# The last block's FFN up projection by seven Strassen products in place of eight, with operands over the mixer's tiles

## The chip, the cores and the metric

One core of one Trainium2 chip. The metric is the device time of one execution in microseconds (us). TensorE (PE) multiplies, PEld is its weight load, VectorE (DVE), ScalarE (ACT) and GpSimd (POOL) work elementwise, SyncE (SP) issues the DMAs.

## What is computed

A hybrid layer for 2048 prompt tokens and 32 tokens of a running stream: input projection, stick-breaking attention beside an SSD scan, an output projection, and a convolutional FFN. The change touches the part after the output projection:

```python
def layer(x, ..., p):
    m, ... = mixer(rmsnorm(x, p['g_mix_pre']), ..., p)      # ends in  @ p['w_out']
    x = x + rmsnorm(m, p['g_mix_post'])
    f, ... = conv_ffn(rmsnorm(x, p['g_ffn_pre']), ffn_conv_prev, p)
    x = x + rmsnorm(f, p['g_ffn_post'])

def conv_ffn(h, conv_prev, p):
    gu = h @ p['w_up']                                      # 1024 -> 2 * 2816
    gate, up = gu[..., :D_FF], gu[..., D_FF:]
    gate_c, conv_new = causal_dwconv(gate, conv_prev, p['ffn_conv_w'], p['ffn_conv_b'])   # width 3
    act = jax.nn.gelu(gate_c, approximate=True) * up
    return act @ p['w_down'], conv_new
```

## The kernel before

Tokens run in four blocks of 512, 512, 512 and 544 (`SBS`; the last has 512 prompt tokens and the 32 of the stream), channels on the 128 partitions. Each fp32 operand is a pair of fp32r tiles, hi (a cast) and lo (the rest, by a subtraction). `dense` (L126) makes a product of 128 by 128 weights with three matmuls: hi with hi, hi with lo, lo with hi. The matmuls of the last block have 272 columns (two token halves), those of the others 512.

After `phase_in` (projections and SSD, all blocks), attention runs block by block, and the work that follows it for block s, `Tail.stream(s)`, is spread as filler between the attention steps of block s + 1; the order on PE is pinned there (`pin`, `mark`). The last block's stream runs alone (`alone`), unpinned, with PSUM pools `t` (3 banks) and `o` (2) and extra pools for loads and weights.

`stream` (L1117) goes so: `out_units` for the first token half, then for the second with steps of `residual(a)` in between (every fourth); `root(a)`; `residual(b)`; `split` of both halves; `root(b)`; the `owed` last downs of the block before; and then 22 pairs `up(s, j)` with `down` after each group of three (four in the last group of the last block). `residual` normalises the projected tile `m` and adds x; the squares for the next root are added on POOL (`square`, L782). `split` makes hi (ACT, L981) and lo (DVE, L982) of the operand with the gain but without the root r; `up` multiplies the gate's and the up half's sums by r (L1015 for the gate). So the matmuls do not wait for the root.

`up` issues 8 x 3 matmuls per token tile for the gate tile j and as many for the up tile 22 + j, so 96 of 272 columns in the last block. Between them stand the convolution and GELU: scale (ACT, L1026), two taps (DVE, L1028), Square (ACT, L1033), a product (DVE, L1034), Sigmoid (ACT, L1035), a product (POOL, L1036); then the product with up (DVE, L1045), and ah (ACT, L1050) and al (POOL, L1051) for the downs. In the last block two small DMAs (`o_fconv`) store the convolution's new state out of the tile `gb`, and the Square overwrites that tile.

`weight` (L97) makes hi and lo of a weight tile of 128 x 1024 in block 0 out of a raw load (`wraw`; ACT cast L110, POOL subtraction L111), and stores both to DRAM (L114, `wS_...`, 1 MiB); later blocks recall them with a DMA (L106). There are two raw tiles (`RBUFS`) and three weight tiles (`WBUFS`). SP issues its DMAs in order, and each waits for the one eight before it.

Of the kernel before, what the change touches and what calls it, by code (L numbers as in the profile page):

```python
# [18 lines left out]
STORE = True  # L19
WBUFS = 3  # L20
RBUFS = 2

P = 128
# [37 lines left out]
class Kernel:  # L61
# [35 lines left out]
    def weight(self, pool, src, n=KC, key=None, tag=None):  # L97

        nc = self.nc
        w = pool.tile([P, 2, KC, P], F32R, name=tag or "w", bufs=1 if tag else self.wbufs)  # L100
        hi, lo = w[:, 0], w[:, 1]
        keys = key if isinstance(key, list) else [key]
        if keys[0] in self.kept:
            m = n // len(keys)
            for i, k in enumerate(keys):
                nc.sync.dma_start(w[:, :, m * i : m * i + m, :].bitcast(F32), self.kept[k][:])  # L106
            return hi, lo
        raw = self.wp.tile([P, KC, P], F32, name="wraw", bufs=RBUFS)
        nc.sync.dma_start(raw[:, :n, :], src)
        nc.scalar.copy(hi[:, :n, :], raw[:, :n, :])  # L110
        nc.gpsimd.tensor_tensor(lo[:, :n, :], raw[:, :n, :], hi[:, :n, :].bitcast(F32), op=ALU.subtract)  # L111
        if key is not None and STORE:
            d = self.kept[key] = self.dp.tile([P, 2, n, P], F32, name="wS_" + "_".join(map(str, key)))
            nc.sync.dma_start(d[:], w[:, :, :n, :].bitcast(F32))  # L114
        return hi, lo
# [4 lines left out]
    def dense(self, ps, w, x, c0, c1, ks=KC, k0=0, first=True, last=True, pin=False):  # L120
        nc = self.nc
        (whi, wlo), (xhi, xlo) = w, x
        at = lambda t, k: t[k] if isinstance(t, list) else t[:, k, :]
        for k in range(ks):
            for i, (l, r) in enumerate(((whi, xhi), (whi, xlo), (wlo, xhi))):
                mm = nc.tensor.matmul(  # L126
                    ps[:, : c1 - c0],
                    l[:, k, :],
                    at(r, k0 + k)[:, c0:c1],
                    start=first and i == 0 and k == 0,  # L130
                    stop=last and i == 2 and k == ks - 1,
# [26 lines left out]
    def rstd_steps(self, pool, psp, pt, sq, n, width, tag="rstd", out=None, rcol=None, of=None, stay=False):  # L158
# [7 lines left out]
        for b in range(nb):  # L166
            q = min(P, n - b * P)
            for i, t in enumerate(sq):
                nc.tensor.matmul(
                    ps[:q, b : b + 1], t[:, b * P : b * P + q], self.ones[:, 0:1],  # L170
                    start=i == 0, stop=i == len(sq) - 1,
                )
# [446 lines left out]
class Attention:  # L619
# [172 lines left out]
    def heads(self, s, steps, every=None):  # L792
# [55 lines left out]

        def values():


            while late:
                h, kc, p, wt, v = late.pop()
                if kc == s and p == 0:
# [469 lines left out]
```

## Time and profile before

| what | us |
|---|---|
| runs: median (lowest to highest) | 2937.53 (2934.23 to 2947.28) |
| profiled execution: span of the core | 2945.7 |
| PE busy in it | 2816.0 (96%) |
| DVE, ACT, POOL busy | 1696.8, 1250.6, 1273.1 |
| mean granted TensorE clock | 0.978 of full |
| DMA | 586.36 MB, mean 199 GB/s |

The times come from separate runs, the profile from one execution of its own; its span is the time from the first instruction to the last, and nothing else is known of that execution's time. Stretches of the span are read as busy time per engine; "the chain of waits" follows back from what ended last.

### The profile page before, as it was taken

The page shows a single profiled execution, that of the slowest core. Times are in us where ns is not written, and L with a number is a line of the kernel's source. Part 1 is how long each engine was busy: PE and PEld are TensorE (multiplying, and loading weights), DVE is VectorE, ACT ScalarE, POOL GpSimd, SP SyncE. Part 2 cuts the span into 40 slices and gives each one's busy share as a digit, 9 for nine tenths or more (in the row PEclk, how much of TensorE's full clock was granted, in tenths as well). Part 3 has the DMA queues.
Part 4 walks back from the last instruction along what each step waited for, and adds up shares of the span by engine and source line. Part 5 has one row for each costly group of instructions (what it writes and reads, how often), then busy time and mean ns, then how long its engine had stood idle before and what let it go on. Part 6 is the DMA issues. An engine that isn't in the chain of part 4 may idle for free.

```text
span 2945.7 us, 44837 instructions
## 1 busy us (share of the span) xinstructions
PE 2816.0 (96%) x16699; PEld 2427.4 (82%) x16699; DVE 1696.8 (58%) x2628; ACT 1250.6 (42%) x2534; POOL 1273.1 (43%) x1083
## 2 busy tenths in 40 slices
PE   8999999989889999999999999999999999999997
PEld 6777787977778888888788888978888889899997
DVE  7667576557774555537644455786666652623333
ACT  4344444337665444436433334664444443311111
POOL 4565555435676656547422222553223234511113
PEclk9999999989999999999999999999999999999998
DMA  5646463648677777777555556656554445755555
GB/s 179 183 143 187 145 173 120 173 131 271 223 266 246 267 266 251 271 261 249 194 190 182 179 171 212 247 175 219 179 175 165 167 160 200 242 183 172 170 183 194
DMA packets 251308, 586.36 MB, mean 199 GB/s; under 512 B 66154, under 2 KB 107762, under 8 KB 222546
## 3 DMA queue, kind: packets, MB, share of 16 engines
q1 hardware_dynamic: 251090, 583.49, 59.9%
q8 instruction: 133, 2.18, 0.3%
q14 instruction: 85, 0.70, 0.1%
HBM read 445.70 MB, written 137.69 MB: 198 GB/s over the span
## 4 chain that ended last, share of the span: by engine, by line
PE 74%; DVE 12%; DMA 7%; ACT 2%; issue 2%; POOL 1%; SPq 1%; DVEq 0%; POOLq 0%; ACTq 0%
PE o L126 36%; PE u L126 12%; PE t L126 11%; PE z L821 4%; PE pa L862 4%; PE pt L840 3%; PE o L370 2%; DVE xc L346 2%; DMA acB<-acD 1%; DVE prow L672 1%; DMA w<-wS_out 1%; DVE acB L446 1%; DVE xc L342 1%; DVE x L268 1%; DMA xr<-hS 1%
## 5 line engine op out<-in xcount | busy, mean ns | idle before, releaser
L126 PE MATMUL o<-xhi,w 128*128 128x512 f32 (+2 forms) x3968 | 1047.4, 346 | 30.1 <-ACT xhi L292 7.7
L126 PEld LDWEIGHTS o<-xhi,w 128*128 128x128 f32 x3968 | 698.2, 192 | 124.2 <-ACT xhi L292 7.7
L126 PE MATMUL o<-xlo,w 128*128 128x512 f32 (+2 forms) x1984 | 683.8, 345 | 6.9 <-DVE xlo L278 4.2
L111 POOL TENSOR_TENSOR w<-wraw,w 128x1024 fp32r<-128x1024 f32 (+2 forms) x156 | 369.0, 2366 | 228.2 <-ACT w L110 207.1
L677 POOL TENSOR_TENSOR beta<-beta,prow 128x512 f32<-128x512 f32 (+3 forms) x256 | 255.0, 998 | 429.1 <-DVE prow L672 345.5
L126 PEld LDWEIGHTS o<-xlo,w 128*128 128x128 f32 x1984 | 380.5, 192 | 51.7 <-DVE xlo L278 6.1
L1036 POOL TENSOR_TENSOR y<-y,gb 128x512 f32<-128x512 f32 (+1 forms) x88 | 115.8, 1317 | 544.4 <-ACT gb L1035 544.4
L126 PE MATMUL u<-xhi,w 128*128 128x512 f32 x1056 | 349.4, 398 | 0.0
L126 PE MATMUL o<-ah,w 128*128 128x512 f32 x992 | 342.5, 403 | 3.1 <-DVE f L1082 3.0
L845 DVE TENSOR_TENSOR wt<-pt,wt 128x512 fp32r<-128x512 f32 (+2 forms) x320 | 191.7, 602 | 156.5 <-ACT wt L844 153.9
L672 DVE TENSOR_TENSOR_SCAN prow<-gam,prow,z 128x513 f32<-128x513 f32 x192 | 245.3, 1277 | 61.5 <-ACT beta L670 58.9
L844 ACT CAST wt<-pt 128x512 fp32r<-128x512 f32 (+2 forms) x320 | 167.5, 526 | 208.7 <-PE pt L840 207.1
L126 PEld LDWEIGHTS u<-xhi,w 128*128 128x128 f32 x1056 | 199.1, 189 | 46.6
L126 PEld LDWEIGHTS o<-ah,w 128*128 128x128 f32 x992 | 187.5, 189 | 45.4 <-DVE f L1082 3.9
L669 ACT ACTIVATE gam<-z 128x512 f32<-128x512 f32 (+2 forms) x320 | 173.3, 542 | 95.5 <-PE z L821 69.8
L126 PE MATMUL u<-xlo,w 128*128 128x512 f32 x528 | 209.4, 397 | 0.0
L110 ACT CAST w<-wraw 128x1024 fp32r<-128x1024 f32 (+2 forms) x156 | 155.2, 995 | 124.7 <-PE o L126 91.3
L1028 DVE SCALAR_TENSOR_TENSOR y<-gb,cv,y 128x512 f32<-128x512 f32 (+1 forms) x176 | 160.0, 910 | 69.2 <-ACT y L1026 66.3
L126 PE MATMUL o<-al,w 128*128 128x512 f32 x496 | 196.8, 397 | 0.0
L126 PE MATMUL t<-xhi,w 128*128 128x272 f32 x960 | 189.1, 292 | 1.7 <-DMA w<-wS_out 1.3
L840 PE MATMUL pt<-ident,beta 128*128 128x128 f32 x1088 | 183.2, 279 | 7.7 <-DVE rn_v L178 4.4
L862 PE MATMUL pa<-wt,v 128*64 128x256 f32 (+3 forms) x1152 | 176.2, 283 | 12.5 <-DVE wt L845 6.9
(269 smaller groups left out, 5086.3 us busy)
## 6 DMA issues: line engine op xcount, KB each, us to landing
w<-wS_up SPq DMA_DIRECT2D x132, 1024.0 KB, 4.8
w<-wS_dn SPq DMA_DIRECT2D x72, 768.0 KB, 4.8
wS_up<-w SPq DMA_DIRECT2D x44, 1024.0 KB, 4.8
w<-wS_out SPq DMA_DIRECT2D x39, 1024.0 KB, 6.7
wraw<-wup SPq DMA_DIRECT2D x44, 512.0 KB, 5.8
k<-kS SPq DMA_DIRECT2D x80, 256.0 KB, 4.3
v<-vS SPq DMA_DIRECT2D x80, 256.0 KB, 4.2
wS_dn<-w SPq DMA_DIRECT2D x24, 768.0 KB, 4.5
```

Source lines behind the costliest of these rows:

```text
L110: nc.scalar.copy(hi[:, :n, :], raw[:, :n, :])
L111: nc.gpsimd.tensor_tensor(lo[:, :n, :], raw[:, :n, :], hi[:, :n, :].bitcast(F32), op=ALU.subtract)
L126: mm = nc.tensor.matmul(ps[:, : c1 - c0], l[:, k, :], at(r, k0 + k)[:, c0:c1], start=first and i == 0 and k == 0, stop=last and i == 2 and ...
L669: nc.scalar.activation(g[:, c0:512], z, AF.Sigmoid, scale=-0.125)
L672: nc.vector.tensor_tensor_scan(back(pr), back(g), z[:, 0:1].to_broadcast([P, n + 1]), self.kn.ones[:, 0:1] if prev is None else prev, op0= ...
L677: eng.tensor_tensor(b[:, :n], b[:, :n], pr[:, c0 + 1 : 513], op=ALU.mult)
L821: mm = nc.tensor.matmul(z[:, :n], q[:, P * b : P * b + P], k[:, :n], start=e == 0, stop=e == 1 and kc < s)
L840: mm = nc.tensor.transpose(t[:, P * j : P * j + P], w[:, P * j : P * j + P], kn.ident[:])
L844: nc.scalar.copy(hi, t)
L845: nc.vector.tensor_tensor(lo, t, hi.bitcast(F32), op=ALU.subtract)
L862: nc.tensor.matmul(av[:m, 2 * P * p + c0 : 2 * P * p + 2 * P], v[:, j, :m], wt[:, rest, j, c0:], start=kc == s and p + j + rest == 0, stop ...
L1028: nc.vector.scalar_tensor_tensor(y[:, :W], gb[:, i : i + W], kn.col(wc + i), y[:, :W], op0=ALU.mult, op1=ALU.add)
```

## The change

1. The last block (`FAST = (3,)`) takes gate tile and up tile of a pair as the two rows of a 2 x 2 block matrix (columns: the two halves of the 1024 input channels), and the token halves as the two columns of the other. Seven products of 4 x 3 matmuls (`pair`) give all four results, with sums of weights on one side and sums of operands on the other (Winograd's form of Strassen). Products 1, 6, 7 and 4 are summed in one PSUM bank (`o`), products 5 and 3 in another; ACT copies the bank out after 1, 6, 7 and 4, and the copies are p1, t and twice u. The first two pairs (`AHEAD`) run products 1 and 2 before the others.

2. The weights' sums are made in block 0 (`sums`: four DVE operations of 128 x 512 per pair, in place in the raw tiles) and stored (L1305, `sS_...`, 88 of 256 KB). In the last block, factors 1, 2 and 4 are recalled as hi and lo, and 7, 5, 6 and 3 are loaded as sums and split again by ACT (L145) and POOL (L146).

3. The operands are scaled with the root ahead of their split: `near` for the first half, `far` for the second, which also makes the sums of operands. So `up`'s product with r goes in that block.

4. In all blocks the operands are written over the mixer's tiles (`self.x = self.cat`). Then root and split of the first half follow its residual as steps during the second half's out-projection (every second step). Squares are summed in pairs of tiles.

5. Weight tiles are halved (`UNIT = 4`: 128 x 512; six of them, five raw). Down weights are loaded by output tile, half as large and twice as many. In the last block the activations are in the pool of kept weights, and the downs of a group start one pair later.

The diff, cut to its core:

```diff
+UNIT = 4
+WBUFS = 6
+RBUFS = 5
+FAST = (3,)
+AHEAD = 2
+OWED = 20
...
+    def sums(self, j, gate, up):
+        (a11, a12), (a21, a22) = gate, up
+        op = lambda out, a, b, o: nc.vector.tensor_tensor(out[:], a[:], b[:], op=o)
+        op(a11, a11, a21, ALU.subtract)
+        op(a21, a21, a22, ALU.add)
+        op(a22, a22, a11, ALU.subtract)
+        op(a12, a12, a22, ALU.subtract)
+        return {7: a11, 5: a21, 6: a22, 3: a12}
...
+    def pair(self, s, j, acts):
...
+        early = j < AHEAD
+        onto = {2: 1, 3: 5, 7: 6} if early else {3: 5, 6: 1, 7: 1, 4: 1}
+        for i in (1, 2, 5, 6, 3, 7, 4) if early else (1, 5, 6, 2, 7, 3, 4):
+            w = self.factor(s, j, i)
+            base = onto.get(i, i)
+            if base == i:
+                ps[i] = self.bank(i, j)
+            b = ps[base]
+            for k in (0, 2):
+                kn.dense(b, w[k : k + 2], self.X[i], 0, h, k0=k, first=base == i and k == 0, ...)
...
+            if i == 1:
+                nc.scalar.copy(p1, b)
+            elif i == 5:
+                nc.scalar.copy(v, b)
+            elif i == 6:
+                add(t, b, p1) if early else nc.scalar.copy(t, b)
+            elif i == 2:
+                nc.scalar.copy(gb[:, 2 : 2 + h], b) if early else add(gb[:, 2 : 2 + h], b, p1)
+            elif i == 3:
+                add(gb[:, 2 + h : 2 + h + e], b[:, :e], t[:, :e])
...
+            elif i == 7:
+                add(u, b, p1) if early else nc.scalar.copy(u, b)
+                nc.gpsimd.tensor_tensor(v, v, u, op=ALU.add)
+            elif early:
+                add(u, u, b)
+            else:
+                nc.scalar.copy(u, b)
...
+            if s == 0 and FAST:
+                for i, t in self.sums(j, *raw).items():
+                    d = self.raws[j, i] = kn.dp.tile([P, 4, P], F32, name=f"sS_{j}_{i}")
+                    nc.sync.dma_start(d[:], t[:])
...
+        self.cat = cat
-        chain = self.residual(s, a)
+        chain = chained(self.residual(s, a), self.ready(s, a))
         for n, _ in enumerate(self.out_units(s, cat, b)):
             yield
-            if n % 4 == 0:
+            if n % 2 == 0:
                 next(chain, None)
-        self.root(s, a)
-        for _ in self.residual(s, b):
+        for _ in chain:
             pass
-        self.split(s, a)
-        self.split(s, b)
-        self.root(s, b)
-        yield from owed
+        self.finished(self.residual(s, b))
+        early = []
+        if fast:
+            yield from islice(owed, OWED)
+            root = kn.rstd_steps(att.tmp, *kn.bank, self.sq, b[1] - b[0], D, stay=True, pin=self.pin)
+            next(root)
+            yield from islice(owed, 4)
+            self.far(s, b, next(root))
+            yield from owed
+            acts = {0: []}
+            early = [self.pair(s, j, acts[0]) for j in range(AHEAD)]
+            for p in early:
+                yield from islice(p, 4)
+        else:
+            self.finished(self.split(s, b))
+            self.finished(self.root(s, b))
+            yield from owed
```

ACT's order in a stretch of the last block's pairs without downs. Before, each pair gives it these six instructions (scale, Square, Sigmoid, two copies for the convolution's edge, and ah):

```order
L1026 ACTIVATE y<-gb,cv 128x546
L1033 ACTIVATE gb<-y 128x546
L1035 ACTIVATE gb<-gb 128x546
L1004 COPY gb<-fhist 128x2
L1006 COPY gb<-cv 128x2
L1050 CAST ah<-y 128x544
```

After, a piece of the same stretch (L1233, L1239, L1241 and L1247 are the scale, Square, Sigmoid and ah; L1206, L1208, L1210, L1221 and L1226 the copies after products 1, 5, 6, 7 and 4; L145 the casts of loaded sums):

```order
L1233 ACTIVATE y<-gb,cv 128x546
L1206 COPY y<-o 128x272
L145 CAST w<-wraw 128x512
L1226 COPY ub<-o 128x272
L1239 ACTIVATE gb<-y 128x546
L1208 COPY ub<-t 128x272
L145 CAST w_26855<-wraw 128x512
L1241 ACTIVATE gb<-gb 128x546
L1210 COPY y<-o 128x272
L145 CAST w_26889<-wraw 128x512
```

PSUM copies and casts of the next pair now stand in front of and behind the Square, which waits for the state's DMA.

POOL's order at the entry into the last block's FFN. Before, behind the power (L188) of the second half's mixer root, adds of squares (L782) and of residuals (L967):

```order
L188 TENSOR_TENSOR rn_v<-rn_v,mhalf 128x3
L782 TENSOR_TENSOR fsq<-fsq,sqt 128x256 x6
L967 TENSOR_TENSOR m_23490<-m_23490,xr 128x272
L782 TENSOR_TENSOR fsq<-fsq,sqt 128x256
L967 TENSOR_TENSOR m_23492<-m_23492,xr 128x272
L782 TENSOR_TENSOR fsq<-fsq,sqt 128x256
```

After, the end of the same stretch, up to the FFN root's power (L226; L824 are the squares, L1037 the sums of pairs of tiles, L146 the splits of weights; the four residual adds, L1025, stand just ahead):

```order
L146 TENSOR_TENSOR w<-wraw,w 128x512 x2
L824 TENSOR_TENSOR fsq<-fsq,sqt 128x256 x2
L1037 TENSOR_TENSOR n_24648<-n_24648 128x544
L146 TENSOR_TENSOR w<-wraw,w 128x512
L824 TENSOR_TENSOR fsq<-fsq,sqt 128x256 x2
L1037 TENSOR_TENSOR n_24648<-n_24648,n_24649 128x544
L146 TENSOR_TENSOR w<-wraw,w 128x512
L146 TENSOR_TENSOR w_25712<-wraw,w_25712 128x512
L824 TENSOR_TENSOR fsq<-fsq,sqt 128x256 x2
L146 TENSOR_TENSOR w_25760<-wraw,w_25760 128x512
L226 TENSOR_TENSOR rn_v<-rn_v,mhalf 128x3
```

Six splits of weights and two wide adds now stand ahead of the power.

SP's order in block 0's FFN. Before, loads and stores alternate:

```order
L114 DMA wS_up_9202<-w 128x2048
L109 DMA wraw<-wup 128x1024
L114 DMA wS_up_9263<-w 128x2048
L109 DMA wraw<-wup 128x1024
L114 DMA wS_up_9328<-w 128x2048
L109 DMA wraw<-wdn 128x768
```

After:

```order
L149 DMA wS_up_0_9426<-w 128x1024
L122 DMA wraw<-wup 128x512 x2
L1305 DMA sS_7_9505<-wraw 128x512
L149 DMA wS_up_4_9431<-w 128x1024
L149 DMA wS_up_0_9494<-w 128x1024
L1305 DMA sS_5_9507<-wraw 128x512
L149 DMA wS_up_4_9499<-w 128x1024
L1305 DMA sS_6_9509<-wraw 128x512
L122 DMA wraw<-wup 128x512
L1305 DMA sS_3_9511<-wraw 128x512
```

The loads of the next pair stand among the stores of this pair's sums.

More of the change, by code (lines that the diff above doesn't have):

```diff
@@ L109, in weight @@
[L109 to L115, printed above, removed]
+        out = []
+        for i in range(0, n, self.unit):
+            m = min(self.unit, n - i)
+            keys = key if isinstance(key, list) else [key and (*key, i)]
+            t = tag and f"{tag}{i}"
+            if keys[0] in self.kept:
+                out += self.recall(pool, keys, m, t)
+            else:
+                out += self.divide(pool, self.raw(src[:, i : i + m, :], m), m, keys[0], t)
@@ new lines, in scale, with near @@
+    def scale(self, half, k, r):
+        m = self.m(k, half)
+        self.kn.nc.vector.scalar_tensor_tensor(
+            m, self.h[k], self.kn.col(C_GFFN + k), r[:, : half[1] - half[0]], op0=ALU.mult, op1=ALU.mult
+        )
+        return m
+    def near(self, s, half):
+        kn, nc, att = self.kn, self.kn.nc, self.att
+        c0, c1 = half
+        r = kn.rstd_narrow(att.tmp, *kn.bank, self.sq, c1 - c0, D, stay=True)
+        yield
+        hi, lo = self.x = self.cat
+        for k in range(KC):
+            self.part(self.scale(half, k, r), hi[k][:, c0:c1], lo[k][:, c0:c1])
+            yield
```

378 lines of the change are left out of this document (282 added, 96 removed).

## The prediction

> **What bounds the kernel now.** I read the table of stretches first: 50 us each, with the busy time of PE, PEld, DVE, ACT and POOL, the granted clock, the DMA share and GB/s.
>
> ```profile
> 1000.00:1050.00 50.00, 50.00 (x236) 40.93 (x236) 25.83 (x31) 22.81 (x42) 30.88 (x21) 1.00 0.76 258
> 1050.00:1100.00 50.00, 50.00 (x242) 40.69 (x241) 28.70 (x35) 24.27 (x45) 29.14 (x18) 1.00 0.80 274
> 2550.00:2600.00 50.00, 44.47 (x341) 44.28 (x341) 16.00 (x32) 12.82 (x30) 10.38 (x9) 0.93 0.64 220
> 2750.00:2800.00 50.00, 50.00 (x400) 50.00 (x400) 17.35 (x40) 9.30 (x18) 8.19 (x6) 1.00 0.50 169
> 2900.00:2945.00 45.00, 30.04 (x219) 28.69 (x217) 18.93 (x49) 8.04 (x18) 20.05 (x24) 0.84 0.64 216
> ```
>
> Inside a stage PE has no idle time at a full clock, in block 0's FFN (the first two rows) and in the last block's (the fourth). Time is lost where stages meet, as in the third row, and at the end. The chain of waits (start, length, what), at the entry into the last block's FFN, then shows what the matmuls cost and which wait ends last.
>
> ```profile
> 2556.12 3.62 PE t L126 x29
> 2559.75 5.53 DMA w<-wS_up
> 2573.28 24.14 PE t L126 x192
> 2597.42 6.02 PE o L126 x48
> ```
>
> 48 matmuls of 272 columns take 6.02 us, 192 take 24.14: 125.6 ns each, back to back. One weight tile was 5.53 us late at the entry. Those are the two numbers that the change can move most.
>
> **The products: -33 us.** Each of the 22 pairs of the last block now issues 7 x 4 x 3 = 84 matmuls of 272 columns where it issued 96. 22 x 12 = 264 fewer, times 125.6 ns: -33.2 us. All of it is on the path, if nothing else becomes the bound there.
>
> **What the stage must carry beside them: +3 us.** A pair's products take 84 x 0.1256 = 10.6 us, with its downs (24 x 2 matmuls a pair) 16.6. New on ACT, POOL and DVE are the splits of four sums per pair and the PSUM copies. The nearest rows (groups by form; mean ns behind the busy time):
>
> ```profile
> L110 ACT CAST w<-wraw 128x1024 fp32r<-128x1024 f32 x124 | 130.3, 1051 | 102.7 <-PE o L126 69.7 <-DMA wraw<-wq 9.9 <-issue 6.8
> L1033 ACT ACTIVATE gb<-y 128x546 f32<-128x546 f32 x22 | 14.6, 662 | 83.8 <-DMA o_fconv<-gb 82.2 <-DVE y L1028 1.6
> L111 POOL TENSOR_TENSOR w<-wraw,w 128x1024 fp32r<-128x1024 f32 x124 | 314.0, 2532 | 214.7 <-ACT w L110 205.2 <-issue 2.8 <-PE z L821 2.5
> L1036 POOL TENSOR_TENSOR y<-y,gb 128x546 f32<-128x546 f32 x22 | 30.0, 1363 | 259.3 <-ACT gb L1035 259.3
> L1051 POOL TENSOR_TENSOR al<-y,ah 128x544 fp32r<-128x544 f32 x22 | 30.1, 1369 | 39.3 <-ACT ah L1050 34.2 <-issue 5.1
> ```
>
> Half tiles at half the duration: POOL per pair 4 x 1.27 + 1.36 + 1.37 and one 272-wide add near 0.8 = 8.6 us, under 10.6. POOL is not the bound. ACT's order is the risk. In 22 executions its Square (L1033) sat idle 82.2 us, 3.7 us each, for the two DMAs that store the convolution's state; in the changed order the copies that empty the PSUM bank (L1226, L1210) stand around and behind that instruction, and product 7 of the next pair may not add to the bank before the copy of product 6 (L1210) is done. Counting from product 3's end: sum 0.44, DMA 4.86 (its row is below), Square 0.66, then Sigmoid 0.66, the copy 0.45 and two casts of 0.5: about 8.1 us. PE reaches that product after some 70 matmuls, 8.8 us. The wait is covered by 0.7 us; a slower DMA or a cast more uncovers it. Between 0 and 10 us for the stage (half a microsecond in each of 20 pairs); I take 3.
>
> **The entry into the last block's FFN: +6 us.** Before, the operands needed only the split, and the root was applied to the products' sums (L1015). Now `near` and `far` scale by the root first, so the products hang on it, and on the sums of operands that `far` makes. The lines below are from the groups of POOL and DVE.
>
> ```profile
> L782 POOL TENSOR_TENSOR fsq<-fsq,sqt 128x256 f32<-128x256 f32 x42 | 33.0, 800 | 3.1 <-ACT sqt L781 2.5
> L1113 POOL TENSOR_TENSOR f<-f,xr 128x256 f32<-128x256 f32 x24 | 20.0, 836 | 28.8 <-DMA xr<-hS 26.6 <-DVE f L1109 2.2
> L963 DVE SCALAR_TENSOR_TENSOR m<-m,cv,u 128x256 f32<-128x256 f32 x48 | 19.3, 473 | 7.5 <-PE u L200 7.5
> ```
>
> Between the two powers (L226) POOL's order holds 10 adds of squares (0.80), 4 residual adds (0.84), 6 weight halves (1.27) and 2 adds of pairs (about 1.3, by L1036): 8.0 + 3.4 + 7.6 + 2.6 = 21.6 us. PE has 30 matmuls of 512 columns and 48 of 272 in that time; the wide ones go at 5.60/24 = 233 ns:
>
> ```profile
> 2000.18 5.60 PE u L126 x24
> ```
>
> 7.0 + 6.0 = 13.0 us, so PE idles up to 8.6 us at the root. Behind it come 8 scalings of 0.47 with casts and subtractions, and the 1088-wide cast (about 1.1) and subtraction (about 1.4) of product 6's operand; 24 early matmuls (3.0 us) cover most, 3 us stay. 11.6 us against the 5.5 us of before's late tile, which has been recalled by then: +6. It is 0 if half of POOL's 21.6 us lies ahead of the root's first input, as it may; +14 if the tile is late all the same and the clock halves. The clock row is this, in stretches of 10 us: the idle stretch has 0.66.
>
> ```profile
> 2560.00:2570.00 10.00, 4.59 (x24) 4.62 (x25) 3.33 (x7) 1.68 (x4) 2.48 (x2) 0.66 0.96 350
> ```
>
> **The end: +3 us.** The chain before:
>
> ```profile
> 2886.76 6.04 PE t L126 x48
> ...
> 2894.04 4.86 DMA o_fconv<-gb
> ...
> 2904.28 1.35 POOL al L1051
> 2905.67 1.01 PE t L126 x6
> ```
>
> From the last gate matmul (2892.80) to the last `al` (2905.63) run 12.8 us, covered by 48 up and 27 down matmuls, 75 x 0.1256 = 9.4. In the changed order 51 stand behind the last product 3, 6.4 us: 3.0 more idle. The last sums need the same chain.
>
> **Block 0: +7 us.** 88 sums on DVE and 88 stores of 256 KB are added. DVE has some 23 of 50 us free there; the nearest op is this, so 88 x 0.74 = 65 us over the 449 us of the FFN's loads is no bound by itself:
>
> ```profile
> L677 DVE TENSOR_TENSOR beta<-beta,prow 128x512 f32<-128x512 f32 x43 | 31.9, 742 | 1.1
> L109 SPq DMA_DIRECT2D wraw<-wup x44: 376/430/2223, 807.3 to 1256.1; - x44
> ```
>
> DMA moves 258 to 274 GB/s at a share of 0.76 to 0.80, so about 340 at full share; 88 x 262 KB in 449 us adds 51: 0.93. It fits, just. What may not is the ring of raw halves: five, of which a pair of tiles holds four until the sums are stored. Issues (KB, median us to landing):
>
> ```profile
> wS_up<-w SPq DMA_DIRECT2D x44, 1024.0 KB, 4.8
> wraw<-wup SPq DMA_DIRECT2D x44, 512.0 KB, 5.8
> k<-kS SPq DMA_DIRECT2D x80, 256.0 KB, 4.3
> ```
>
> One turn: load 4.3, cast 0.5, subtraction 1.27, two sums 1.5, store 4.3 = 11.9 us with the 256-KB row; load 5.8, cast 0.5, two subtractions 2.5, three sums 2.2, store 4.8 = 15.8 with the longer ones. PE needs a pair every 48 x 0.233 / 0.82 = 13.6 us (the FFN's 22 x 72 matmuls of 233 ns are 369 of the 449 us). The middle, 13.8, is even; between 0 and 52 us (below), I take half a microsecond in each of the 15 pairs that directly follow another: +7.
>
> The Trainium skill ("DMA: Bandwidth & Descriptors", "Bandwidth") asks for transfers of at least 1 MiB and speaks against halving them; its fit of 2.0 us and bytes/436 GB/s ("Anatomy of one DMA") would make, as an estimate, 2.6 us for 256 KB, a turn of 8.5 us, so +0 here and 2910 in the end. The rows of this trace, 4.3 to 5.8, contradict the fit, and the sum goes by them.
>
> **The chain moved into the second half's out-projection: -6 us.** The first half's residual ran in steps among the second half's out-projection; its root and split came after the last matmul, with those of the second half. Now they are steps of the same chain. A stretch of 10 us at such a place, and the split's row:
>
> ```profile
> 1370.00:1380.00 10.00, 6.52 (x32) 5.10 (x31) 10.00 (x17) 9.26 (x24) 7.75 (x10) 0.89 0.62 186
> L982 DVE SCALAR_TENSOR_TENSOR xlo<-m,cv,xhi 128x256 fp32r<-128x256 f32 x48 | 32.1, 712 | 2.0 <-DMA y<-xT 1.7 <-ACT xhi L981 0.3
> ```
>
> PE lost 3.5 us of ten with DVE full; 16 splits of 0.71 are 11.4 us of DVE in one go, and half of them leave that place. Between 0 and -10 (three such places); I take 2 each.
>
> **Sum.** -33.2 + 3 + 6 + 3 + 7 - 6 = -20.2 against the profiled span of 2945.7 us. That span lies 8.2 above the median of the runs, 2937.5 (2934.2 to 2947.3); the same difference against the median gives 2917.
>
> **Rivals.**
>
> *The ring of raw halves starves PE in block 0 (slower).* A DVE sum that runs beside a POOL split may take far longer than 0.74 us. The timeline (start, length), and the line's min/median/max:
>
> ```profile
> 1077.19 2.41 POOL L111 TENSOR_TENSOR w<-wraw,w 128x1024 fp32r<-128x1024 f32 x1 [3.68 <-ACT w L110]
> 1077.90 2.25 DVE L1028 SCALAR_TENSOR_TENSOR y<-gb,cv,y 128x512 f32<-128x512 f32 x1 [1.20 <-ACT y L1026]
> L1028 DVE SCALAR_TENSOR_TENSOR y<-gb,cv,y x176: 726/752/2250, 888.9 to 2895.1; 128x512 f32<-128x512 f32 x132, 128x546 f32<-128x546 f32 x44
> ```
>
> An op of 0.75 took 2.25, until the split beside it was over. One sum held for a half split adds 1.27 to a turn of 15.8: 17.1, 3.5 above 13.6, in 15 pairs 52 us. In place of my 7: 2962. It is slower than the bound from a turn of 16.5 on. For it: the loads stand in SP's order behind the stores. Against it: the downs between groups of pairs give back time, and every other row of the turn must be at its long end. The Trainium skill states the mechanism ("SBUF — State Buffer", "Who interferes with whom"): a DVE instruction with two SBUF inputs and a GpSimd instruction that reads SBUF share a port, and who issues first keeps it; these two rows agree.
>
> *The gain is eaten (no change).* ACT waits for the state's DMA in each pair (+10 in place of 3), the entry costs 14 and nothing comes back in blocks 0 to 2: -33.2 + 10 + 14 + 3 + 7 + 0 = +0.8, 2938. For it: 3.7 us of ACT idleness per pair is there already. Against: the covers, small as they are.
>
> *Better.* Entry, stage and block 0 at their low ends, the moved chain at its high one: -33.2 + 3 - 10 = -40, 2897.
>
> **How the numbers follow.** Forecast 0.53, eaten 0.22, ring 0.17, better 0.08. A measurement of this kernel can tell 0.5%, 14.7 us, from no change. Faster: 0.53 + 0.08, less 0.04 for a forecast that ends above 2922.8: 0.57. Same: 0.22 + 0.04 = 0.26. Slower 0.17. The forecast's own range is 2900 to 2930; the range of 2895 to 2958 takes in the eaten gain and most of the ring, and leaves out some 0.15.
>
> **What would show it.** Right: 84 matmuls of 272 columns at 125.6 ns per pair, PE 50 of 50 and a clock of 1.00 between 2600 and 2850; PE idle 8 to 14 us at the root of the last block; block 0's FFN still 50 of 50. Wrong: PE waiting in block 0 for weights (a split or a raw load) between 900 and 1250; PE waiting in each pair of the last block for ACT's L1210 or L1226; or a root that costs under 5 us.

## The result, and the profile after

2977.4 us (2972.3 to 2979.9), against 2940.1 for the kernel before: slower by 1.1%, ratio 1.0113 (1.0084 to 1.0142). I had forecast 2917, with a range that ended at 2958. The medians differ by 37.3 us, the profiled spans (2974.7 and 2945.7) by 29.0: the profiled execution before was longer than its median, the one after a little shorter.

The table of stretches of the changed kernel, 50 us each, with the columns of the prediction:

```profile
1000.00:1050.00 50.00, 48.59 (x234) 39.04 (x234) 36.47 (x45) 22.56 (x48) 30.60 (x26) 1.00 0.87 313
1050.00:1100.00 50.00, 48.31 (x237) 39.47 (x238) 35.22 (x44) 25.05 (x53) 32.06 (x28) 1.00 0.84 289
2550.00:2600.00 50.00, 31.11 (x205) 28.96 (x203) 38.17 (x53) 18.94 (x39) 39.32 (x37) 0.83 0.52 163
2750.00:2800.00 50.00, 49.18 (x393) 48.97 (x392) 21.14 (x41) 20.05 (x43) 27.94 (x21) 1.00 0.70 222
2900.00:2950.00 50.00, 44.95 (x344) 44.15 (x343) 15.60 (x33) 15.31 (x32) 18.28 (x18) 0.93 0.56 176
```

Two places differ. In block 0's FFN (first two rows) PE is no longer full and DVE has gone from 26 to 36 of 50. At the last block's entry (third row) PE has 31 of 50 at a clock of 0.83, with DVE and POOL near 40. (The entry stands some 30 us later here than in the trace before, so the third rows of the two tables are not quite the same place.) The pairs behind it (fourth row) run almost as forecast: PE has 49.2 of 50, and the chain's pieces have 27 matmuls in 3.37 us, 125 ns each.

```profile
2702.38 3.37 PE t L161 x27
2722.28 3.01 PE o L161 x24
```

Products on DVE's timeline (before's L1015, now L1279, the gate's sum by r) mark stretches that both traces have.

- From block 2's 22nd gate product (2418.57 before, 2449.10 after) to the end of the span: 527.1 us before, 525.6 after. The last block thus keeps 1.5 of the 33 us that its products save. PE's idle time there, up to its last matmul, went from 16.8 to 40.3 us; the rest went with the slower clock.
- From block 0's first gate product to its 22nd: 389.5 us before, 407.2 after. Of the 17.7 us, 8.5 are idle time of PE, which had none there before. The others are work that has moved: some 40 attention matmuls more fall into the stretch (453, before 412), and 48 fewer into the one ahead of it from block 0's first output-projection load on (571, before 619).
- Since work moves from stretch to stretch, the cost of block 0 is better read over a longer one, from that first load (`wraw<-wout`, at 671.1 before, 675.5 after) to block 2's 22nd gate product: 1747.5 us before, 1773.6 after, 26.1 more. I call it the long stretch.

In block 0 the sums' group on DVE, with what ended the idle time before them, and one sum beside a run of POOL's splits:

```profile
L1134 DVE TENSOR_TENSOR wraw<-wraw 128x512 f32<-128x512 f32 x88 | 92.3, 1048 | 49.9 <-POOL w L146 23.0 <-DMA wraw<-wup 20.0 <-issue 5.3
```

```profile
1038.81 6.16 POOL L146 TENSOR_TENSOR w<-wraw,w 128x512 fp32r<-128x512 f32 x4
```

```profile
1042.32 1.77 DVE L1134 TENSOR_TENSOR wraw<-wraw 128x512 f32<-128x512 f32 x1 [1.19 <-POOL w L146]
```

A sum takes 1.05 us in the mean, not 0.74: 92 us of DVE, and 50 more of waits at the head of its order. In this trace the 21 sums during which POOL did nothing took 0.68 us in the mean, the 52 beside a split 1.28. PE waits in the FFN (us in total, times, longest) for the products that stand behind the sums, which empty the up bank:

```profile
PE u L161 <- DVE y L1313: 6.4, 5, 3.0
PE o L161 <- DVE f L1348: 1.3, 2, 1.0
```

The longest of these waits: a sum waits for a raw load, the product of the up bank stands behind it, and PE waits for the product.

```profile
1101.53 1.22 DVE L1134 TENSOR_TENSOR wraw<-wraw 128x512 f32<-128x512 f32 x1 [2.82 <-DMA wraw<-wup]
1102.67 0.68 DVE L1313 TENSOR_TENSOR y<-u,y 128x512 f32<-128x512 f32 x1
1103.49 0.47 PE L161 MATMUL u<-xhi,w 128*128 128x512 f32 x1 [2.99 <-DVE y L1313]
```

Seven of the 88 sums stand ahead of the first gate product (888.2), from 841.9 us on. There two of them wait for POOL's splits in front of a product of attention (L887) for which PE waits:

```profile
847.62 3.41 DVE L1134 TENSOR_TENSOR wraw<-wraw 128x512 f32<-128x512 f32 x2 [4.19 <-POOL w L146]
850.95 0.68 DVE L887 TENSOR_TENSOR wt<-pt,wt 128x512 fp32r<-128x512 f32 x1
851.69 0.66 PE L882 MATMUL pt<-ident,beta 128*128 128x128 f32 x4 [3.65 <-DVE wt L887]
```

In the run without sums and stores (below) PE waits 0.31 us at that place.

At the entry, the chain of waits goes through POOL:

```profile
2552.58 3.01 POOL w L146 x2
2555.59 1.36 POOL fsq L824 x2
2556.95 1.22 POOL w L146
2558.17 0.83 POOL rn_v L226
2559.05 1.48 PE u L238 x6
2560.55 3.36 DVE n L1077 x8
```

Splits of weights stand ahead of the power, as in the prediction: POOL works from 2536.9 to the power at 2558.1, 21.2 us, where I had added up 21.6. PE's waits there (in brackets), and what DVE had in the last two of them:

```profile
2554.61 1.21 PE L203 MATMUL u<-ones,n 128*128 128x1 f32 x12 [2.84 <-DVE n L1037]
2559.05 1.47 PE L238 MATMUL u<-ident,rn_v 128*128 128x128 f32 x6 [3.23 <-POOL rn_v L226]
2564.05 0.98 PE L203 MATMUL u<-ones,fsq 128*128 128x1 f32 x4 [3.54 <-POOL xlo L1073]
2582.93 3.19 PE L161 MATMUL o<-n,w 128*128 128x272 f32 x13 [4.00 <-DVE y L1186]
2606.43 0.59 PE L161 MATMUL o<-xhi,w 128*128 128x272 f32 x1 [8.72 <-DVE ub L1186]
```

```profile
2573.69 7.97 DVE L1380 SCALAR_TENSOR_TENSOR f<-f,cv,fsq 128x256 f32<-128x256 f32 x8
2594.88 7.84 DVE L1380 SCALAR_TENSOR_TENSOR f<-f,cv,fsq 128x256 f32<-128x256 f32 x8 [1.51 <-ACT fsq L248]
2605.95 0.43 DVE L1186 TENSOR_TENSOR ub<-o,y 128x272 f32<-128x272 f32 x1
```

Eight scalings in a row (the finish of block 2, the normalisation of that block's FFN output, which the prediction did not mention) stand in DVE's order ahead of the adds L1186 that empty the first pairs' banks. The trace before has them too, in the same place and 2 us shorter, but from 2540 to 2600 PE waited there for nothing of DVE:

```profile
2540.61 5.82 DVE L1109 SCALAR_TENSOR_TENSOR f<-f,cv,rstd 128x256 f32<-128x256 f32 x8
2550.77 5.69 DVE L1109 SCALAR_TENSOR_TENSOR f<-f,cv,rstd 128x256 f32<-128x256 f32 x8 [0.28 <-ACT rstd L206]
```

The clock, in stretches of 10 us, is below full where PE idled:

```profile
2549.00:2559.00 10.00, 3.98 (x35) 3.68 (x33) 1.98 (x3) 3.87 (x10) 10.00 (x11) 0.84 0.49 164
2559.00:2569.00 10.00, 5.84 (x23) 5.36 (x24) 8.45 (x15) 3.95 (x10) 8.47 (x10) 0.50 0.43 133
2599.00:2609.00 10.00, 2.57 (x11) 2.57 (x12) 9.28 (x13) 1.67 (x3) 7.17 (x7) 0.56 0.62 212
```

### The profile page after: what moved, and what is told of

Same layout as the page of the kernel before. It is cut to its first block, busy times and chain, and to the rows that moved or that the text cites. A ratio compares the mean times of both kernels' runs of the same rounds, so it can differ in the third digit from the quotient of the medians.

```text
span 2974.7 us, 46718 instructions
## 1 busy us (share of the span) xinstructions
PE 2803.0 (94%) x16507; PEld 2410.4 (81%) x16507; DVE 1804.9 (61%) x2711; ACT 1345.0 (45%) x2817; POOL 1452.4 (49%) x1253
## 4 chain that ended last, share of the span: by engine, by line
PE 51%; DVE 5%; DMA 4%; POOL 2%; issue 2%; ACT 1%; SPq 0%; DVEq 0%; POOLq 0%; ACTq 0%
PE o L161 24%; PE u L161 10%; PE t L161 8%; PE pa L904 3%; PE z L863 3%; PE pt L882 3%; DMA xr<-hS 1%; DVE prow L714 1%; DMA w<-wS_out 1%; POOL w L146 1%; DMA o_fconv<-gb 1%; DMA wraw<-wup 1%; DMA sS<-wraw 0%; PE u L203 0%; DVE xlo L1052 0%
## 5 line engine op out<-in xcount | busy, mean ns | idle before, releaser
L161 PE MATMUL o<-xhi,w 128*128 128x512 f32 (+2 forms) x3424 | 947.0, 355 | 36.2 <-DVE ub L1186 8.7
L161 PEld LDWEIGHTS o<-xhi,w 128*128 128x128 f32 x3424 | 614.5, 192 | 131.5 <-issue 10.8
L146 POOL TENSOR_TENSOR w<-wraw,w 128x512 fp32r<-128x512 f32 (+3 forms) x332 | 522.4, 1580 | 298.8 <-ACT w L145 270.5
L161 PE MATMUL o<-xlo,w 128*128 128x512 f32 (+2 forms) x1712 | 607.5, 355 | 5.6 <-DVE xlo L320 3.6
L719 POOL TENSOR_TENSOR beta<-beta,prow 128x512 f32<-128x512 f32 (+3 forms) x256 | 261.0, 1020 | 454.1 <-DVE prow L714 362.2
L161 PEld LDWEIGHTS o<-xlo,w 128*128 128x128 f32 x1712 | 329.6, 193 | 50.8 <-DVE xlo L320 5.3
L145 ACT CAST w<-wraw 128x512 fp32r<-128x512 f32 (+3 forms) x332 | 226.5, 684 | 171.4 <-PE o L161 48.7
L887 DVE TENSOR_TENSOR wt<-pt,wt 128x512 fp32r<-128x512 f32 (+2 forms) x320 | 191.1, 601 | 140.9 <-ACT wt L886 138.8
L1300 POOL TENSOR_TENSOR y<-y,gb 128x512 f32<-128x512 f32 x66 | 87.0, 1318 | 269.4 <-ACT gb L1299 265.4
L904 PEld LDWEIGHTS pa<-wt,v 128*64 128x64 f32 (+1 forms) x1152 | 152.0, 167 | 26.1 <-DVE wt L887 9.6
L712 ACT ACTIVATE beta<-z 128x512 f32<-128x512 f32 (+2 forms) x320 | 172.1, 538 | 0.0
```

Of the source, the lines that this page charges most:

```text
L145: nc.scalar.copy(hi, raw[:, :m, :])
L146: nc.gpsimd.tensor_tensor(lo, raw[:, :m, :], hi.bitcast(F32), op=ALU.subtract)
L161: mm = nc.tensor.matmul(ps[:, : c1 - c0], l, r, start=first and i == 0 and k == 0, stop=last and i == 2 and k == len(w) - 1, **({"skip_gro ...
L712: nc.scalar.activation(b[:, :n], z, AF.Sigmoid, scale=0.125)
L719: eng.tensor_tensor(b[:, :n], b[:, :n], pr[:, c0 + 1 : 513], op=ALU.mult)
L887: nc.vector.tensor_tensor(lo, t, hi.bitcast(F32), op=ALU.subtract)
```

## The experiments

Each time is a median; ratios are to the kernel before, measured beside it (2939.9 to 2944.4). Edits are against the changed kernel unless said, and cut to their core. The expectations call the stretch of 385.3 us in block 0 (before: 366.2) one to the 22nd gate product; it ends at the 20th. Numbers below go to the 22nd.

**1. The parts of the change.**

Without the products:

```diff
-FAST = (3,)
+FAST = ()
```

> FAST = (): no Strassen products, no sums, no stores of sums; half weight tiles, operands over the mixer's tiles and the moved chain stay. The changed kernel's profile is 29.0 us longer than before's, which I put down to four places: block 0's FFN +15, the transition from block 1 to block 2 +11, the entry into the last block's FFN with its slower clock about +28, the end and the rest some +8, against the -33 of the products. Theory: the transition 1 to 2 belongs to the part that stays here, the other costs go with the products: 2940 + 11 = about 2951, and the stretch from block 0's first gate product to the 22nd at 366 to 368 us as before. Rival: the halved tiles and the twice as many DMAs are what slowed block 0: that stretch stays above 380 us, and the time is about 2966. Second rival: the parts that stay are neutral, 2940.

2939.6 us, ratio 0.9994 (0.9975 to 1.0013). The second rival holds: halved tiles, operands over the mixer's tiles and the moved chain are neutral together. The transition from block 0 to block 1 (22nd gate product to the next) fell from 126.6 to 115.2 us, but block 1's stretch of gate products rose from 418.3 to 428.2, and block 1's 22nd to block 2's 22nd from 598.3 to 607.7. All of the loss belongs to the products, their sums and stores.

Without the sums:

```diff
-        op(a11, a11, a21, ALU.subtract)
-        op(a21, a21, a22, ALU.add)
-        op(a22, a22, a11, ALU.subtract)
-        op(a12, a12, a22, ALU.subtract)
```

> The four DVE sums of a pair are left out in block 0; what is stored and split again in the last block is the raw halves (the up projection of the last block computes other values; its instructions are the same). All DMAs, stores of 256 KB included, stay. Theory: in block 0 the sums stand in DVE's order and wait there for raw loads (20.0 us of DVE's idle time) and for POOL's splits (23.0 us), and the product that empties the up bank (L1313) stands behind them; PE's 8.4 us of idleness and the attention work that slips go with the sums. The stretch from the first to the 22nd gate product falls from 385.3 to 367 to 371 us, the time to about 2960. Rival: DMA (share 0.82 to 0.92, up to 318 GB/s) makes the raw loads late: the stretch stays at 380 or more, the time at 2972 to 2977.

2954.7 us, ratio 1.0042 (1.0027 to 1.0058): the sums cost 22.8 us by the medians, with some 10 either way by the intervals, and 23.1 in the long stretch (1750.5). Block 0's stretch is 389.3, as before, and PE is full although DMA is as busy as with the sums:

```profile
1000.00:1050.00 50.00, 50.00 (x240) 40.83 (x239) 24.46 (x32) 24.29 (x50) 31.59 (x28) 1.00 0.88 316
```

So DMA is not what starved PE there.

Without sums and stores:

```diff
-            for i, t in self.sums(j, *raw).items():
-                d = self.raws[j, i] = kn.dp.tile([P, 4, P], F32, name=f"sS_{j}_{i}")
-                nc.sync.dma_start(d[:], t[:])
+            for i, (c, k) in {7: (j, 0), 5: (NJ + j, 0), 6: (NJ + j, 4), 3: (j, 4)}.items():
+                self.raws[j, i] = kn.a["wup"][c][:, k : k + 4, :]
```

> Neither sums nor their stores in block 0; the last block loads raw halves of the weights in their place (other values in the last block's up projection, the same instructions there). Both theories of block 0 expect the stretch at 366 to 369 us and about 2960; against the run without sums alone it shows what the 88 stores cost: 0 to 2 us by the theory of DVE's order, 12 or more by the rival of DMA.

2940.2 us, ratio 0.9993 (0.9976 to 1.0010): the stores cost 14.4 more (some 7 either way; 11.2 in the long stretch, 1739.3), against my 0 to 2. Block 0's stretch is 387.0, so only 2 us of them lie in it; the transition to block 1 differs by 11 (125.9 with the stores, 115.0 without). Why there, the runs do not settle. And the last block's products gain nothing: this run equals the one without products, and its last stretch (524.5 us) that of the one without products (524.9).

**2. What in the sums costs.**

As much DVE time without waits (four subtractions of a 128x48 tile of its own per sum; raw halves stored):

```diff
+                for _ in range(4):
+                    nc.vector.tensor_tensor(z, z, z, op=ALU.subtract)
```

> The 88 sums of block 0 are replaced by as much DVE time that waits for nothing: four subtractions of 128x48 on a small resident tile each (about 0.7 us in all); raw halves are stored as they are, as in the run without sums (2954.7 us; the last block computes other values). Theory: the sums cost by waiting at the head of DVE's order for raw loads (20.0 us of idleness) and splits (23.0 us): without the waits 2955 to 2960. Rival: it is the DVE time itself, or the port it shares with POOL's splits (sums of 1.78 us beside a split, 0.69 alone): 2968 to 2977.

3016.9 us, ratio 1.0267, worse than with the sums. It is no clean test:

```profile
L1309 DVE TENSOR_TENSOR dummy<-dummy x352: 174/208/1308, 782.5 to 1013.5; 128x48 f32<-128x48 f32 x176
L1309 DVE TENSOR_TENSOR dummy<-dummy 128x48 f32<-128x48 f32 x352 | 137.9, 392 | 9.4
```

The subtractions took 137.9 us, half as much again as the 92.3 of the sums, and the order put all 352 into 231 us, up to 38 in a row. What it does show is that work on DVE can hold PE up without a wait of its own: these wait for nothing, and PE waited 15.6 us for the product of the up bank. How much of the 23 us of the sums is of this kind, it can't tell.

The sums behind that product, same work and place:

```diff
+        kn.tc.add_manual_dep(op(a11, a11, a21, ALU.subtract).ins, self.prod.ins.name, ..., reason="late")
```

> The sums stay in block 0, but each pair's four stand in DVE's order behind the product that empties its up bank (L1313) instead of ahead of it. The run without sums is at 2954.7 us, the changed kernel at 2977.4. Theory: what costs 23 us is that L1313 stands behind a sum which waits for a raw load or a split: 2955 to 2962. Rival: DVE's time and the port: 2970 to 2977. Second rival: the raw tiles are held longer, the next loads come late and PE waits for ACT's and POOL's splits of weights: above 2977.

3102.0 us, ratio 1.0535. The second rival holds: the raw tiles are kept until the pair's end, and PE waits for casts of raw loads.

```profile
PE o L161 <- ACT w L145: 81.6, 18, 6.8
```

Four raw halves in place of five, and its control without the products:

```diff
-RBUFS = 5
+RBUFS = 4
```

> The changed kernel with four raw halves in place of five. Theory: the ring of raw halves binds block 0 (a pair holds four of them until its sums are stored; with the sums behind the up product the time was 3102 us, and PE waited 81.6 us for casts of raw loads): with no fifth buffer the next pair's first load waits for a store of this pair's sums, 1.5 to 4 us more in each of 22 pairs: 3010 to 3060. Rival: DVE's time and the port cost the 23 us, and the ring has room: 2972 to 2985.

> Control to the run before: no Strassen products, no sums, four raw halves in place of five. Without sums a raw half is free once it is split: 2938 to 2943, as with five (2939.6). If it is 2950 or more, four raw halves bind by themselves and the run before tells nothing about the sums.

2981.6 and 2932.1 us. My theory of the ring falls in the size that I gave it: one buffer fewer costs 4 us with the sums, not 33 or more. But without products and sums it gains 7, so the fifth buffer may be worth some 12 us to the products, sums and stores, about as much as the intervals leave open. The ring is not the main cost of the changed kernel; that it has no part in it isn't shown.

The sums in block 1, from raw halves loaded again:

```diff
-        if s == 0 and FAST:
+        if s == 1 and FAST:
+            raw = [[kn.raw(kn.a["wup"][c][:, i : i + UNIT, :], UNIT) for i in (0, UNIT)] for c in (j, NJ + j)]
```

> The sums are made in block 1, where DVE is busy for 24 of 50 us, POOL for 11 and DMA moves 170 GB/s: four raw halves per pair are loaded a second time there, summed on DVE, stored. Block 0 is then as in the run without sums and stores (2940.2 us). Theory: what cost 37 us in block 0 was the place, DVE's order behind late raw loads and POOL's splits and a DMA near its limit; here the raw tiles are used for nothing else and no split stands in between: 2940 to 2947. Rival: the sums and stores cost by themselves, 23 and 14 us wherever they stand: 2965 or more.

2944.5 us, ratio 1.0014 (1.0003 to 1.0026): sums and stores cost 4 us there, no more than the intervals allow for, with 23 MB more to read.

**3. The last block's entry.**

The finish of block 2 behind the second pair's last product (its first matmul pinned there, its steps started at pair 2):

```diff
+                    if fast and j < AHEAD:
+                        continue
+                    if fast and j == AHEAD and i == 0:
+                        kn.mark(kn.lastmm)
                     if j and i % 2:
                         next(done, None)
```

> The finish of the block before (two times eight scalings of 128x256 on DVE, 7.97 and 7.84 us in one row, with their adds) is put behind the last product of the second pair, where it stood between the first two pairs' adds. Theory: those rows stand in DVE's order ahead of the adds that empty the first pairs' PSUM banks; PE's waits of 4.00 and 8.72 us for L1186 go, and the slower clock behind them: 12 to 18 us, 2960 to 2965. Rival: the root and the operands of the second half set when the products can run, and other waits take their place: 2972 to 2977. A part may come back later, where the 8 us rows stand ahead of a gate add: up to 4 us.

2981.1 us, ratio 1.0121: nothing gained. The waits of 4.00 and 8.72 are gone, and others have come:

```profile
2570.32 0.82 PE L161 MATMUL t<-xhi,w 128*128 128x272 f32 x2 [4.54 <-ACT xhi L1073]
2580.15 2.18 PE L161 MATMUL o<-n,w 128*128 128x272 f32 x8 [3.21 <-DVE n L1074]
2622.70 1.22 PE L239 MATMUL u<-ident,rn_v 128*128 128x128 f32 x4 [3.29 <-POOL rn_v L227]
2637.31 0.59 PE L161 MATMUL t<-w,w 128*128 128x272 f32 x1 [3.47 <-ACT w L1248]
```

The root out of the operands (gain alone; r at the gate's sums):

```diff
-            m, self.h[k], self.kn.col(C_GFFN + k), r[:, : half[1] - half[0]], op0=ALU.mult, op1=ALU.mult
+        self.kn.nc.scalar.activation(m, self.h[k], AF.Copy, scale=self.kn.col(C_GFFN + k))
...
+        nc.vector.tensor_tensor(gb[:, 2:514], gb[:, 2:514], self.r[:, :512], op=ALU.mult)
```

> In the last block the operands of the products are scaled by the gain alone (on ACT), and the root is applied to the gate's sums in each pair by two more DVE products (546 wide in all), as before did. So no product waits for a root; the sums of block 0 stay. The run without sums and stores, 2940.2 us, equals the run without Strassen, 2939.6: the 33 us of the products are lost in the last block itself, where PE is idle for 40.3 us from the 22nd gate product of block 2 on (before: 16.7) and the clock falls to 0.50 to 0.85 in six stretches of 10 us. Theory: the chain root, scaling, split, sums starts this (waits of 2.84, 3.23 and 3.54 us at the root, each a step in which PE has nothing to do): without the root in it PE's idle time in the last block falls by 8 to 12 us, the clock's loss with it, 2977 to about 2963. Rival: elementwise work as such is the limit at the entry (DVE 9.8 of 10 us, POOL 8 to 10), as the run with the later finish says, where other waits took the same time: 2972 or more.

2975.9 us, ratio 1.0126; with the sums in block 1 as well:

> Both edits of the two runs before this one: root applied at the gate, sums made in block 1. If the two theories hold and add: 2940 to 2947 less 14, 2926 to 2933, faster than the kernel before (2941) by 0.3 to 0.5%. If elementwise work limits the entry: 2940 to 2947. If the sums cost by themselves: above 2955.

2952.8 us, 8 more than with the sums in block 1 alone. The theory's gain didn't come, as the rival said. But the edit tests it in part only: it takes the root out of the operands and leaves the root's own matmuls in PE's order ahead of the products. In the first of the two runs PE waits longer there than before the edit (2.84 us), for the sums of squares, and later for an add of the first pairs:

```profile
2551.06 2.03 PE L203 MATMUL u<-ones,n 128*128 128x1 f32 x12 [7.67 <-DVE n L1037]
2584.73 3.09 PE L161 MATMUL o<-n,w 128*128 128x272 f32 x12 [4.58 <-DVE y L1183]
```

POOL and ACT free of splits in the last block (sums made and split in block 1, recalled as hi and lo), then the later finish too:

```diff
+                kn.divide(kn.wp, t, UNIT, ("sum", j, i))
...
-        return kn.divide(pool, kn.raw(self.raws[j, i][:], 4), 4, None, tag)
+        return kn.recall(pool, [("sum", j, i)], 4, tag)
```

> Sums in block 1 as in the run with that edit (2944.5 us), and split there too (ACT, POOL); hi and lo are stored (88 of 512 KB) and recalled in the last block, so that POOL and ACT make no splits of weights there. In the changed kernel's entry POOL works without a gap from 2536.9 to 2560.0, with six splits of weights (some 8.7 us) in front of the power (2558.13) that PE's L238 waits for. Theory: POOL's order is what makes the root late; without the splits PE's idleness of 2.8 + 3.2 + 3.5 us at the root goes and with it some of the slower clock, 8 to 12 us: 2933 to 2937, a little faster than the kernel before (2941.5). Rival: DVE's queue (waits of 4.0 and 8.7 us for the adds of the first pairs) takes back what the root gives: 2942 to 2946. Second rival: the larger recalls (3.5 to 4.6 MB per pair) bind in the last block: above 2950.

> The run before with the finish of the block before put behind the second pair. In the changed kernel that edit alone gained nothing (2981 against 2977): the wait moved. Theory of elementwise work as the limit at the entry: with POOL's splits gone there is room behind the second pair, and the two edits together take the waits of 4.0 and 8.7 us too: 2922 to 2930. Rival: the finish costs the same wherever it stands: as the run before or up to 4 us more.

2969.9 and 2963.9 us in all, but the last block's stretch (block 2's 22nd gate product to the end) fell from 527.9 (sums in block 1) to 515.7 and 509.1: the splits on POOL and ACT in the last block are worth 12 us, and with them away the later finish is worth 7, where alone it was worth nothing. In the second of them, from the root's wait on:

```profile
2553.87 0.84 PE L239 MATMUL u<-ident,rn_v 128*128 128x128 f32 x6 [1.77 <-POOL rn_v L227]
2559.26 0.82 PE L161 MATMUL t<-xhi,w 128*128 128x272 f32 x2 [4.55 <-ACT xhi L1073]
2574.22 4.65 PE L161 MATMUL o<-n,w 128*128 128x272 f32 x35 [0.69 <-DVE n L1074]
```

Block 1 pays for it: from block 0's first to block 2's 22nd gate product 1576 us against 1536.

Half of these pairs in block 2, with the later finish (against the run before):

```diff
-        if s == 1 and FAST:
+        if s == (1 if j < NJ // 2 else 2) and FAST:
```

> Sums and their splits for half of the pairs in block 1, for the other half in block 2; recalled as hi and lo in the last block; the finish of the block before behind the second pair. In the two runs with all of it in block 1 the last block's stretch (from the 22nd gate product of block 2 to the end) fell from 527.9 us (sums in block 1, split in the last block) to 515.7 and, with the later finish, 509.1, but block 1 moved 280 to 330 GB/s at a DMA share of 0.83 to 0.97 and lost 40 us. Theory: spread over two blocks the DMA share stays near 0.75 and the last block's gain is kept: 2925 to 2932, faster than the kernel before (2943). Rival: POOL's, ACT's and DVE's extra work in the attention blocks costs as much there as in one block, since it stands in the attention chain's orders: 2950 to 2965.

2952.8 us (stretch 516.8), in the rival's range: from block 0's first to block 2's 22nd gate product the two blocks pay 26 us more than with the sums alone (1562.8 against 1536.4), where one paid 38. The first four pairs alone split in block 1 (their sums recalled as hi and lo), then the later finish, then four raw halves too:

```diff
+                if j < 4:
+                    kn.divide(kn.wp, t, UNIT, ("sum", j, i))
+                    continue
```

> Sums in block 1 for all pairs as in the run at 2944.5 us; only the first four pairs' sums are split and stored as hi and lo there (16 of 88), the other pairs load sums and split them in the last block as the change does. Theory: what the entry needs is POOL free of splits for the first pairs; block 1 then carries 16 splits in place of 88 (those cost it 40 us): last block's stretch 516 to 520 us (527.9 with all splits there), 2932 to 2937. Rival: the splits of later pairs move up into POOL's order at the entry: stretch 525 or more, 2943 or more.

> As the run before, with the finish of the block before behind the second pair, which took another 7 us from the last block's stretch where no splits stood in the way. Theory: 2926 to 2932, faster than the kernel before (2942). Rival: the finish meets the splits of the pairs from the fifth on, and the wait moves as it did in the changed kernel: 2935 to 2945.

> As the run before with four raw halves in place of five, which took 7 us from the kernel without Strassen (2932.1 against 2939.6). If that gain is the order's and holds here: 7 us less than the run before. If the last block's loads of sums need the fifth raw half: slower than the run before by 5 us or more.

2950.6, 2941.7 and 2951.5 us, stretches of 523.2, 514.6 and 516.3. The splits of the first four pairs are worth 5 of the 12 us, less than the theory said. The later finish is worth 9 us here too. Four raw halves cost 10 with the products where they gained 7 without. In the traces the transition to block 1 and block 1's gate products grew by 9 together, the last block's stretch by 2: it isn't mainly the last block's loads that need the fifth. The best with products is 1.0011 (0.9996 to 1.0026) of the kernel before: no change. Only the control of the ring, without products, is a little below it: 0.9970 (0.9954 to 0.9985).

## Why the prediction was wrong, point by point

**Products, -33:** right. 84 matmuls a pair at 125 ns, and the pairs behind the entry run at a full clock.

**The stage, +3:** small, as forecast, but not for my reason. In the 260 us from 2640 on PE was idle for 1.2 us, for the downs' adds (1.1); the wait for ACT's copies that I had priced didn't come.

**The end, +3:** right in kind. PE's idle time from 2900 on, up to its last matmul, rose from 6.8 to 8.9 us.

**Block 0, +7: the first step that failed.** It measured 37: 22.8 for the sums, 14.4 for their stores. The step that was wrong is "88 x 0.74 = 65 us ... is no bound by itself". I priced a sum at 0.74 us and dismissed DVE because of its free share; a sum took 1.05, and 50 us of waits in DVE's order came on top, in front of products for which PE waits. I looked for the danger in the ring of raw halves. The rival had the place and the sign right and named the wrong cause: in the FFN PE waited 6.4 us for the up bank to be emptied and 0.5 for a weight. The stores were costed only as a share of DMA ("It fits, just"); why they cost what they do stays open.

The Trainium skill ("SBUF — State Buffer", "Who interferes with whom") says that such a sum and a POOL subtraction share a port. The trace agrees: 1.28 us in the mean beside a split, 0.68 with POOL idle. I had this in the rival and left it out of the sum. How much of the 23 us is the port, how much the waits and how much the plain DVE time, the runs do not tell apart.

**The entry, +6: the second step that failed.** The last block's stretch became shorter by 1.5 only, so the entry cost 33.2 - 1.5 less 1.2 for the stage and 2.1 for the end, about 28 us; 20 of them are idle time of PE, which from block 2's 22nd gate product to 2640 was 10.0 us in the trace before and 30.3 after. POOL's late root is there as worked out: PE's waits from 2551 to 2574 are 12.1 us (2.84, 3.23 and 3.54 shown above and three short ones), and I had 11.6. What I left out: the finish of block 2 lies in the same 60 us on the same DVE, and the first pairs' banks now need DVE adds; the two waits for L1186 are 12.7 us. The runs bring back 12 us by taking the splits away and 7 more by the later finish, 19 of the 28; where the others lie stays open. I also took before's late weight tile as a credit of 5.5; the run without products, with the same halved tiles, waits only 3.7 us for such tiles (2.0 and 1.7), so little was to be had.

**The moved chain, -6:** at one transition 11 us came back, and they were lost again in blocks 1 and 2; the whole is 0. No run parts the moved chain from the halved tiles, so what it is worth by itself isn't shown.

**The rivals.** "The gain is eaten" was right for the last block, through the entry and not through the state's DMA; that its 2938 is close to the 2940 of the run without sums and stores is luck. The ring was right in its sign for block 0. Both came at once, and I had given each its chance as though the other stayed away: the range ended short of their sum.

**The halved transfers:** the Trainium skill's rule against them ("DMA: Bandwidth & Descriptors", "Bandwidth") found no cost to explain here: with halved tiles and no products the time did not change. My sentence that the rows contradict the fit was too strong: the Trainium skill gives the fit ("Anatomy of one DMA") for transfers issued by GpSimd. These are issued by SP, so the rows speak for their own path alone.

## What to carry to other kernels

An engine with half its time free is no cover for work that waits: look at what stands behind each new instruction in that engine's order, and price it with the row of the same operation beside the same neighbour. Where a stage begins, add up the elementwise work of both stages that meet there; removing one wait from such a place gives nothing until the engine behind it has room too. Work prepared for a later stage costs what its place costs: the same sums and their stores cost 37 us in block 0 and 4 in block 1. And where work of two kinds is interleaved, a stretch between two events of one kind can grow because work of the other has moved into it: look at PE's idle time in it, and at a stretch long enough to hold both.

## What was not expected of the hardware

The granted clock stood at 0.50 over 10 us in which PE was busy for 5.84 of them, and the matmuls of 272 columns started 0.23 us apart there, 0.126 at a full clock: a part of what PE lost in waits at the entry was lost again by the matmuls behind them. Of the 33.2 us of the products the last block kept 1.5; some 24 more went into PE's idle time, and some 8 are left (33.2 less 1.5 less 23.5). The clock's rows account for most of these: summed over the time in which PE was busy there, the missing share of the clock came to 8.7 us before and to 14.3 after.

The same eight scalings of 128x256 took 5.82 us in the trace before, 7.97 and 7.84 at the crowded entry, and 5.82 again in the run with no splits on POOL there and the later finish.
